# Decay rows of a chunked delta rule: broadcast transfers and a select on GpSimd in place of two bf16 matmuls

## The chip, the cores and the metric

The kernel runs on one core of a Trainium2 chip. Its time is the device time of one execution in microseconds (us). Three timed runs gave 1241.6, 1245.53 and 1245.56 us, so the median is 1245.53 us. One further execution was recorded by the hardware profiler, and all lines of the profile come from that one.

## The reference

One encoder layer on 1024 tokens of width 1024, all in float32. A normalised input goes through one projection, whose columns feed two groups of heads: windowed attention (8 heads) and a gated delta rule (4 heads of 128, run forward and backward over the sequence). Their outputs are concatenated, projected back and added to the input; then follow a squared-ReLU feed-forward block of width 4096 and a last norm. The change lies in the delta rule, which is computed in chunks:

```python
gc = jnp.cumsum(g, axis=-1)
decay = jnp.exp(jnp.where(causal, gc[..., :, None] - gc[..., None, :], -jnp.inf))
kk = jnp.einsum("bnhcd,bnhsd->bnhcs", k, k)
a_mat = jnp.where(strict, beta[..., :, None] * kk * decay, 0.0)
...
qk = jnp.einsum("bnhcd,bnhsd->bnhcs", q, k) * decay
```

So each chunk, head and direction needs a square matrix `decay`: the exponential of a cumulated log-decay of one token less that of another, zero on one side of the diagonal. The kernel uses chunks of 128 tokens.

## The kernel before

**The pieces.** The layer is one long program without loops at run time. `phases` calls generators, and `weave` merges two of them by weights, so that the work of one stands in program order between the work of the other. The order in which each engine gets its instructions is then worked out at build time, by a timeline simulation of the framework (`schedule_with_timeline_sim=True` where the kernel is built). Each engine executes its own list strictly in that order, and waits at an instruction whose inputs or buffers are not ready.

**Buffers.** Tiles are handed out from rings by tag. `pt` has 12 buffers of 128 x 512, `pg` 24 of 128 x 1024, `sc` 4, `wh` and `wl` 3 each for split weights. The PSUM tags `psA` and `psB` have 4 banks each: GEMM results go to `psA`, small products and transposes to `psB`.

**GEMMs.** `gemm` multiplies in three fp32r passes (L127 to L129), 24 matmuls of 128 x 512 for one result bank. The weights are split into a high part by ScalarE (L122) and a low part by GpSimd (L123). The results of the convolved projections are copied out of `psA` by ScalarE (L395), those of `proj_z` by a Silu on ScalarE (L464).

**The stage of the change.** After the k and q projections, `phases` weaves two streams:

```python
run(weave((chain(self.proj_conv(C_GV, "v"), self.proj_z(), self.proj_attn()), 145.0),
          (chain(self.prep(), self.eliminate(), self.diag_blocks(), self.invert(tt, (0, 1))), 100.0)))
```

The first is nothing but GEMMs with what follows them: the v heads with their five-tap convolution on VectorE (L374, L376), a Silu (L378) and transposes on TensorE (L415, drained by L455), then z, then the attention's k, v and q (L477, L488, L500 to L502). The second is `prep`: for each of 8 chunks `c` it makes the 4 heads' k-k and k-q products in two `psB` banks (L637, L639), and for each direction `d` a half step follows:

- two bf16 matmuls put the decay rows on all partitions, in a third `psB` bank `rows`: one with a selector `selb` against `grow`, which holds each cumulated row as three bf16 parts (L644), one that adds the mask of -1e30 through a bf16 identity (L645);
- ScalarE takes four exponentials with a per-partition bias from `rows` into `dec`, a `pt` tile (L649);
- VectorE makes `at` (also `pt`) from `dec` and the k-k product (L653), and ScalarE copies its diagonal blocks into `diag` (L658); `at` goes to DRAM by SyncE's queue (L660);
- VectorE multiplies `dec` by the k-q product (L661), and that goes to DRAM too (L662).

`eliminate` then works on all diagonal blocks with VectorE alone (L670 to L681), `diag_blocks` transposes (L690, L691), and `invert` multiplies the blocks together (its tiles are cleared by L716). After this weave come the attention, the scan and the feed-forward block.

**Where the rows come from.** At the end of `gates`, the cumulated log-decays are transposed into PSUM (L353), cut into three bf16 parts by ScalarE and VectorE (L356 to L361), written to the DRAM tensor `gcd` (L365) and read back into `grow` (L366). `setup2` makes the selector, the identity and the two masks on GpSimd (L168 to L177).

Of the kernel before, what the change touches and what calls it, by code (L numbers as in the profile page):

```python
# [11 lines left out]
BF16 = mybir.dt.bfloat16  # L12
AF = mybir.ActivationFunctionType
ALU = mybir.AluOpType
AX = mybir.AxisListType

P = 128
# [5 lines left out]
GH = 4  # L23
# [5 lines left out]
NEG = -1e30  # L29
# [48 lines left out]
class Block:  # L78
# [76 lines left out]
    def setup2(self):  # L155
        nc, io, c = self.nc, self.io, self.const
        t = lambda name, shape, dt=F32: c.tile(list(shape), dt, name=name)
        ones = t("ones", (P, P))
        nc.gpsimd.memset(ones, 1.0)
        self.ones = ones  # L160
        self.tri = []
        for d, (cm, step) in enumerate(((-1, 1), (1, -1))):
            u = t(f"tri{d}", (P, P))
            nc.gpsimd.affine_select(out=u, in_=ones, pattern=[[step, P]], compare_op=ALU.is_ge, fill=0.0,
                                    base=0, channel_multiplier=cm)
            self.tri.append(u)
        self.identb = t("identb", (P, P), BF16)
        nc.gpsimd.tensor_copy(out=self.identb, in_=self.ident)  # L168
        self.maskb = []
        for d in range(2):  # L170
            m = t(f"maskb{d}", (P, P), BF16)
            nc.gpsimd.tensor_scalar(out=m, in0=self.tri[d], scalar1=-1.0, scalar2=-NEG, op0=ALU.add, op1=ALU.mult)
            self.maskb.append(m)
        self.selb, self.zero = t("selb", (P, 16), BF16), t("zero", (P, 1))
        nc.gpsimd.memset(self.zero, 0.0)
        nc.gpsimd.tensor_tensor(out=self.selb, in0=self.ident[:, 0:16], in1=self.ident[:, 16:32], op=ALU.add)
        nc.gpsimd.tensor_tensor(out=self.selb, in0=self.selb, in1=self.ident[:, 32:48], op=ALU.add)  # L177
        self.dtb = t("dtb", (P, 8))
        nc.sync.dma_start(out=self.dtb, in_=io["gdn_dt_bias"].rearrange("o d h -> o (d h)").to_broadcast([P, 8]))
        self.alog = t("alog", (P, 8))  # L180
        nc.sync.dma_start(out=self.alog, in_=io["gdn_a_log"].rearrange("o d h -> o (d h)").to_broadcast([P, 8]))
        self.nsink = t("nsink", (P, 8))
        nc.sync.dma_start(out=self.nsink, in_=io["attn_sink"].to_broadcast([P, 8]))
        nc.gpsimd.tensor_scalar(out=self.nsink, in0=self.nsink, scalar1=-1.0, scalar2=None, op0=ALU.mult)
        self.ssk, self.irk, self.rk2 = (self.head.tile([P, GH, NT], F32, name=n) for n in ("ssk", "irk", "rk2"))
        self.ssq = t("ssq", (P, GH, NT))
# [118 lines left out]
    def gates(self, ps):  # L305

        nc = self.nc
        c = self.const
        mk = lambda name: c.tile([P, NT, 8], F32, name=name)
        tmp = lambda: self.small((P, NT, 8), bufs=6, tag="gt")  # L310
        vt = nc.vector
# [7 lines left out]
        au, z, z2, p = tmp(), tmp(), tmp(), tmp()  # L319
# [31 lines left out]

        tp = self.ps("psB", (64, P))
        nc.tensor.transpose(tp, gc2.rearrange("p c x -> p (c x)"), self.ident)  # L353
        rr = self.sc((64, 2, P))
        part = self.small((64, 3, P), bufs=1, tag="gparts", dt=BF16)
        nc.scalar.copy(out=part[:, 0, :], in_=tp)  # L356
        vt.tensor_copy(out=rr[:, 0, :], in_=part[:, 0, :])
        vt.tensor_tensor(out=rr[:, 1, :], in0=tp, in1=rr[:, 0, :], op=ALU.subtract)
        vt.tensor_copy(out=part[:, 1, :], in_=rr[:, 1, :])
        vt.tensor_copy(out=rr[:, 0, :], in_=part[:, 1, :])  # L360
        vt.tensor_tensor(out=part[:, 2, :], in0=rr[:, 1, :], in1=rr[:, 0, :], op=ALU.subtract)  # L361
        self.grow = c.tile([P, GH, P], BF16, name="grow")
        nc.gpsimd.memset(self.grow, 0.0)
        for r in range(3):
            nc.sync.dma_start(out=self.gcd[r], in_=part[:, r, :])  # L365
        nc.sync.dma_start(out=self.grow[0:48], in_=self.gcd.rearrange("r (a h) t -> (r a) h t", h=GH))  # L366
        self.cc, self.w2 = mk("cc"), mk("w2")

    def conv_silu(self, ct, raw, out):
# [260 lines left out]
    def prep(self):  # L630
        nc = self.nc
        self.diag = [self.pg((P, 32, 32)) for _ in range(2)]
        for c in range(NT):
            sl = slice(c * P, (c + 1) * P)
            gg, kq = self.ps("psB", (P, GH, P)), self.ps("psB", (P, GH, P))
            for h in range(GH):
                nc.tensor.matmul(gg[:, h, :], self.kT[h][:, sl], self.kT[h][:, sl], start=True, stop=True)  # L637
            for h in range(GH):
                nc.tensor.matmul(kq[:, h, :], self.kT[h][:, sl], self.qT[h][:, sl], start=True, stop=True)  # L639
            for d in range(2):  # L640
                dec, at = self.pt((P, GH, P)), self.pt((P, GH, P))
                rows = self.ps("psB", (P, GH, P))
                i = 2 * c + d
                nc.tensor.matmul(rows, self.selb[:, i:i + 1].to_broadcast([P, P]), self.grow, start=True, stop=False)  # L644
                nc.tensor.matmul(rows, self.identb, self.maskb[d].unsqueeze(1).to_broadcast([P, GH, P]),  # L645
                                 start=False, stop=True)
                for h in range(GH):
                    i = 4 * d + h
                    nc.scalar.activation(out=dec[:, h, :], in_=rows[:, h, :], func=AF.Exp,  # L649
                                         bias=self.ngc[:, c, i:i + 1])  # L650
                for h in range(GH):
                    i = 4 * d + h
                    nc.vector.scalar_tensor_tensor(out=at[:, h, :], in0=dec[:, h, :],  # L653
                                                   scalar=self.cc[:, c, i:i + 1], in1=gg[:, h, :],
                                                   op0=ALU.mult, op1=ALU.mult)
                for q in range(4):
                    r = slice(32 * q, 32 * q + 32)
                    nc.scalar.copy(out=self.diag[d][r, :, 4 * c:4 * c + 4].rearrange("p i h -> p h i"),  # L658
                                   in_=at[r, :, r])
                nc.sync.dma_start(out=self.atd[c, :, d], in_=at)  # L660
                nc.vector.tensor_tensor(out=dec, in0=dec, in1=kq, op=ALU.mult)  # L661
                nc.sync.dma_start(out=self.pd[c, :, d], in_=dec)  # L662
                yield 1.5
# [585 lines left out]
    def build(self):  # L1249
        tc, nc = self.tc, self.nc  # L1250
        with (
# [7 lines left out]
            d = lambda name, shape: dram.tile(list(shape), F32, name=name)  # L1259
            self.biasd = d("biasd", (8, 32, 512))[:]  # L1260
            self.hd, self.sd = d("hd", (NT, P, D))[:], d("sd", (DFF // 256, 7, P, HALF))[:]
            self.gcd = dram.tile([3, 64, P], BF16, name="gcd")[:]
            self.zd, self.mad = d("zd", (GH, P, SEQ))[:], d("mad", (NT, P, HALF))[:]
            self.qad = d("qad", (2, 4, P, SEQ))[:]
            self.ktd, self.qtd = d("ktd", (GH, P, SEQ))[:], d("qtd", (GH, P, SEQ))[:]
# [127 lines left out]
```

## Time and profile before

| | |
|---|---|
| runs | 1241.6, 1245.53, 1245.56 us |
| profiled execution | 1245.29 us, of which the span of the records is 1243.6 us |
| mean granted TensorE clock | 0.983 |
| TensorE matmul busy | 1179.3 us (95% of the span) |
| VectorE, ScalarE, GpSimd busy | 854.0, 620.9, 574.4 us |
| the 32 row matmuls L644 and L645 | first at 144.3, last at 213.1 us |
| the 64 exponentials L649 | first at 145.7, last at 216.1 us |

In the profile, PE is the matmul stream of TensorE and PEld its weight loads, DVE is VectorE, ACT ScalarE, POOL GpSimd and SP SyncE, which here issues most transfers. A queue's name with a q (SPq, ACTq) is the sequencer of that engine. `L644` is a line of the kernel file. Busy time of PE runs a little over, since matmuls overlap in the pipeline: the distance from start to start says what one costs.

### The profile page before, as it was taken

The numbers are of one execution on the slowest core, as the hardware profiler recorded it, in microseconds if no ns is written. First come the engines' busy times: TensorE is split into PE (matmuls) and PEld (weight loads), VectorE is DVE, ScalarE is ACT, GpSimd is POOL, SyncE is SP. The second block draws the span as 40 slices with busy tenths as digits, with TensorE's granted clock in tenths as the row PEclk, the third lists the DMA queues.
The fourth block names the chain that finished last, engine by engine and source line by source line (L and its number), as shares of the span: only waits on it lengthen the run. The fifth ranks groups of instructions, "written<-read, shape, count | busy, mean of one in ns | idle before, by whom it ended". The sixth has DMA issues, their size and how long they took to land. (4 is left out here: it accounts for less than half of the span.)

```text
span 1243.6 us, 18468 instructions
## 1 busy us (share of the span) xinstructions
PE 1179.3 (95%) x6482; PEld 962.8 (77%) x6482; DVE 854.0 (69%) x1466; ACT 620.9 (50%) x1347; POOL 574.4 (46%) x486
## 2 busy tenths in 40 slices
PE   6999999899879999997899999999999999999997
PEld 5788877778657778876788888888777888888885
DVE  4677667973378996677654453544579797887976
ACT  6455688354575752125464544545555433444343
POOL 5354312224422334234474535445365655665595
PEclk9999999899889999998999999999999999999999
DMA  6134344524746667222234444344679624434323
GB/s 240 52 117 141 104 167 140 180 81 135 172 145 172 168 220 263 96 83 84 86 120 154 151 153 144 144 158 147 214 263 320 235 84 155 152 133 138 98 89 136
DMA packets 121629, 187.62 MB, mean 151 GB/s; under 512 B 11043, under 2 KB 64416, under 8 KB 121537
## 3 DMA queue, kind: packets, MB, share of 16 engines
q1 hardware_dynamic: 96708, 152.58, 37.2%
q10 hardware_dynamic: 16381, 29.67, 6.2%
q0 software_dynamic: 8448, 4.20, 2.0%
q8 instruction: 51, 0.84, 0.3%
q14 instruction: 41, 0.34, 0.1%
HBM read 122.39 MB, written 63.49 MB: 149 GB/s over the span
## 5 line engine op out<-in xcount | busy, mean ns | idle before, releaser
L127 PE MATMUL psA<-pg,wh 128*128 128x512 f32 x416 | 164.8, 397 | 1.7 <-ACT pt L464 1.7
L129 PE MATMUL psA<-pg,wl 128*128 128x512 f32 x416 | 164.1, 395 | 0.0
L128 PE MATMUL psA<-pg,wh 128*128 128x512 f32 x416 | 163.7, 394 | 0.0
L123 POOL TENSOR_TENSOR wl<-wr,wh 128x512 fp32r<-128x512 f32 x44 | 66.7, 1536 | 159.6 <-ACT wh L122 129.4
L1168 DVE TENSOR_TENSOR pg<-pg 128x512 fp32r<-128x512 f32 x112 | 123.0, 1133 | 17.6 <-ACT pg L1167 17.6
L123 POOL TENSOR_TENSOR wh<-wr,wh 128x512 fp32r<-128x512 f32 x32 | 47.4, 1502 | 129.0 <-ACT wh L122 129.0
L128 PE MATMUL psA<-pg,pg 128*128 128x512 f32 x256 | 99.9, 392 | 0.4 <-POOL pg L123 0.3
L127 PE MATMUL psA<-pg,pg 128*128 128x512 f32 x256 | 99.3, 392 | 0.9 <-DVE pg L1213 0.9
L1085 ACT ACTIVATE pt<-pt 128x512 f32<-128x512 f32 x64 | 40.3, 632 | 119.3 <-DVE pt L1075 119.3
L129 PE MATMUL psA<-pg,pg 128*128 128x512 f32 x256 | 99.7, 390 | 0.0
L123 POOL TENSOR_TENSOR pg<-wr,pg 128x512 fp32r<-128x512 f32 x48 | 73.4, 1560 | 51.5 <-ACT pg L122 51.5
L127 PEld LDWEIGHTS psA<-pg,wh 128*128 128x128 f32 x416 | 78.6, 189 | 19.0 <-ACT pt L464 2.1
L128 PEld LDWEIGHTS psA<-pg,wh 128*128 128x128 f32 x416 | 78.6, 189 | 17.8 <-issue 0.9
L129 PEld LDWEIGHTS psA<-pg,wl 128*128 128x128 f32 x416 | 78.6, 189 | 16.8
L1167 ACT CAST pg<-pg 128x512 fp32r<-128x512 f32 x112 | 67.1, 620 | 40.4 <-DMA pg<-sd 29.3
L128 PE MATMUL psB<-pg,pg 128*128 128x512 f32 x192 | 74.9, 390 | 0.8 <-POOL pg L123 0.7
L129 PE MATMUL psB<-pg,pg 128*128 128x512 f32 x192 | 74.8, 390 | 0.2 <-DVE pg L1168 0.2
L127 PE MATMUL psB<-pg,pg 128*128 128x512 f32 x192 | 74.7, 389 | 0.0
L122 ACT CAST wh<-wr 128x512 fp32r<-128x512 f32 x76 | 43.6, 623 | 50.0 <-PE psA L128 30.0
L1075 DVE TENSOR_TENSOR pt<-psB,pt 128x512 f32<-128x512 f32 x39 | 26.9, 689 | 54.0 <-PE psB L129 29.5
L1075 DVE TENSOR_TENSOR pt<-psA,pt 128x512 f32<-128x512 f32 x39 | 26.8, 689 | 51.8 <-PE psA L129 36.3
L127 PEld LDWEIGHTS psA<-pg,pg 128*128 128x128 f32 x256 | 48.1, 188 | 12.6 <-DVE pg L1213 2.1
(395 smaller groups left out, 3265.3 us busy)
## 6 DMA issues: line engine op xcount, KB each, us to landing
sd<-pt ACTq DMA_DIRECT2D x112, 256.0 KB, 2.1
pg<-sd SPq DMA_DIRECT2D x112, 256.0 KB, 2.9
wr<-in_w_ffn_in SPq DMA_DIRECT2D x32, 512.0 KB, 3.6
wr<-in_w_in SPq DMA_DIRECT2D x22, 512.0 KB, 5.0
pg<-in_x SPq DMA_DIRECT2D x16, 512.0 KB, 6.7
wr<-in_w_ffn_out SPq DMA_DIRECT2D x16, 512.0 KB, 4.7
sc<-kvd SPq DMA_DIRECT2D x14, 512.0 KB, 6.0
kvd<-pt SPq DMA_DIRECT2D x16, 256.0 KB, 2.4
```

What stands on the lines that cost most here:

```text
L122: nc.scalar.copy(out=h, in_=raw)
L123: (eng or nc.gpsimd).tensor_tensor(out=l, in0=raw, in1=h.bitcast(F32), op=ALU.subtract)
L127: nc.tensor.matmul(ps, wh, xh, start=first, stop=False, skip_group_check=onto)
L128: nc.tensor.matmul(ps, wh, xl, start=False, stop=False, skip_group_check=onto)
L129: nc.tensor.matmul(ps, wl, xh, start=False, stop=last, skip_group_check=onto)
L1075: self.nc.vector.tensor_tensor(out=out, in0=in0, in1=in1, op=ALU.add)
L1085: self.nc.scalar.activation(out=c, in_=c, func=AF.Relu)
L1167: nc.scalar.copy(out=s[:, 0], in_=raw)
L1168: v.tensor_tensor(out=s[:, 1], in0=raw, in1=s[:, 0].bitcast(F32), op=ALU.subtract)
```

## The change

The masks, the bf16 identity, the selector and the tensor `grow` go away, and so does the cutting into three parts. The cumulated rows go to DRAM as they are, in float32. In each half step of `prep`, SyncE issues a transfer that reads the four heads' rows of one chunk and direction (2 KB) and writes them to all 128 partitions of `dec` (256 KB); GpSimd's `affine_select` then replaces one side of the diagonal by -1e30 in place, for the four heads in one instruction of 128 x 512; and the four exponentials work in place on `dec` in SBUF instead of reading PSUM. No third `psB` bank is used.

```diff
 def setup2
-        self.identb = t("identb", (P, P), BF16)
-        nc.gpsimd.tensor_copy(out=self.identb, in_=self.ident)
-        self.maskb = []
-        for d in range(2):
-            m = t(f"maskb{d}", (P, P), BF16)
-            nc.gpsimd.tensor_scalar(out=m, in0=self.tri[d], scalar1=-1.0, scalar2=-NEG, op0=ALU.add, op1=ALU.mult)
-            self.maskb.append(m)
-        self.selb, self.zero = t("selb", (P, 16), BF16), t("zero", (P, 1))
+        self.zero = t("zero", (P, 1))
         nc.gpsimd.memset(self.zero, 0.0)
-        nc.gpsimd.tensor_tensor(out=self.selb, in0=self.ident[:, 0:16], in1=self.ident[:, 16:32], op=ALU.add)
-        nc.gpsimd.tensor_tensor(out=self.selb, in0=self.selb, in1=self.ident[:, 32:48], op=ALU.add)
 def gates
         tp = self.ps("psB", (64, P))
         nc.tensor.transpose(tp, gc2.rearrange("p c x -> p (c x)"), self.ident)
-        rr = self.sc((64, 2, P))
-        part = self.small((64, 3, P), bufs=1, tag="gparts", dt=BF16)
-        nc.scalar.copy(out=part[:, 0, :], in_=tp)
-        vt.tensor_copy(out=rr[:, 0, :], in_=part[:, 0, :])
-        vt.tensor_tensor(out=rr[:, 1, :], in0=tp, in1=rr[:, 0, :], op=ALU.subtract)
-        vt.tensor_copy(out=part[:, 1, :], in_=rr[:, 1, :])
-        vt.tensor_copy(out=rr[:, 0, :], in_=part[:, 1, :])
-        vt.tensor_tensor(out=part[:, 2, :], in0=rr[:, 1, :], in1=rr[:, 0, :], op=ALU.subtract)
-        self.grow = c.tile([P, GH, P], BF16, name="grow")
-        nc.gpsimd.memset(self.grow, 0.0)
-        for r in range(3):
-            nc.sync.dma_start(out=self.gcd[r], in_=part[:, r, :])
-        nc.sync.dma_start(out=self.grow[0:48], in_=self.gcd.rearrange("r (a h) t -> (r a) h t", h=GH))
+        rr = self.small((64, P), bufs=1, tag="grows")
+        vt.tensor_copy(out=rr, in_=tp)
+        nc.sync.dma_start(out=self.gcd, in_=rr)
 def prep
             for d in range(2):
                 dec, at = self.pt((P, GH, P)), self.pt((P, GH, P))
-                rows = self.ps("psB", (P, GH, P))
-                i = 2 * c + d
-                nc.tensor.matmul(rows, self.selb[:, i:i + 1].to_broadcast([P, P]), self.grow, start=True, stop=False)
-                nc.tensor.matmul(rows, self.identb, self.maskb[d].unsqueeze(1).to_broadcast([P, GH, P]),
-                                 start=False, stop=True)
+                i = 4 * (2 * c + d)
+                src = self.gcd[i:i + 4].rearrange("(o h) t -> o (h t)", o=1)
+                nc.sync.dma_start(out=dec.rearrange("p h t -> p (h t)"), in_=src.to_broadcast([P, GH * P]))
+                nc.gpsimd.affine_select(out=dec, in_=dec, pattern=[[0, GH], [-1 if d else 1, P]],
+                                        compare_op=ALU.is_ge, fill=NEG, base=0, channel_multiplier=1 if d else -1)
                 for h in range(GH):
                     i = 4 * d + h
-                    nc.scalar.activation(out=dec[:, h, :], in_=rows[:, h, :], func=AF.Exp,
+                    nc.scalar.activation(out=dec[:, h, :], in_=dec[:, h, :], func=AF.Exp,
                                          bias=self.ngc[:, c, i:i + 1])
 def build
-            self.gcd = dram.tile([3, 64, P], BF16, name="gcd")[:]
+            self.gcd = d("gcd", (64, P))[:]
```

## The prediction

> **What bounds the kernel now.** I read the page's head first, then the busy time by stretches around the change.
>
> ```profile
> span 1243.6 us, 18468 instructions
> PE 1179.3 (95%) x6482; PEld 962.8 (77%) x6482; DVE 854.0 (69%) x1466; ACT 620.9 (50%) x1347; POOL 574.4 (46%) x486
> core 0: us, PE busy (x) PEld busy (x) DVE busy (x) ACT busy (x) POOL busy (x), PEclk, DMA share, GB/s
> 143.00:222.00 79.00, 74.82 (x400) 60.15 (x398) 59.77 (x108) 69.58 (x160) 23.30 (x20) 0.98 0.51 165
> 222.00:262.00 40.00, 39.26 (x166) 32.37 (x167) 37.81 (x68) 5.58 (x11) 4.45 (x3) 0.95 0.32 108
> 262.00:300.00 38.00, 35.43 (x562) 28.50 (x561) 18.56 (x28) 26.61 (x44) 16.26 (x17) 1.00 0.37 118
> 300.00:320.00 20.00, 20.00 (x89) 16.54 (x89) 3.08 (x5) 6.20 (x10) 10.48 (x9) 1.00 0.68 175
> ```
>
> TensorE is the bound of the kernel (95%), but not of every stage alike. In the stage of `prep` (143 to 222 us) ScalarE is busy 69.58 of 79 us, 88%, and TensorE idles 4.2 us. From 222 on ScalarE has little to do, VectorE runs the elimination (37.81 of 40 us), and TensorE is full with the GEMMs of z and the attention: they, not the elimination, set the end of the weave, for 300 to 320 us holds 20.00 us of TensorE after the first inversions are done. The next stage waits for them:
>
> ```profile
> 328.08 2.53 ACT L720 COPY pg<-sc 32x256 f32<-32x256 f32 x4 [6.01 <-POOL pg L716]
> ```
>
> L720 stood 6.01 us for a `pg` buffer's clearing, and `pg` is full of the GEMMs' operands until they end. So a microsecond that TensorE gains before 322 us is a microsecond of the kernel, as long as TensorE is not then stopped by something else. What would stop it is seen where the stage of `prep` ends:
>
> ```profile
> 219.93 1.12 PE L415 MATMUL psB<-ident,sc 128*128 128x128 f32 x4 [1.71 <-DVE pt L661]
> 222.74 0.79 PE L127 MATMUL psA<-pg,wh 128*128 128x512 f32 x1 [1.69 <-ACT pt L464]
> 223.33 0.63 PE L128 MATMUL psA<-pg,wh 128*128 128x512 f32 x1
> 223.75 0.63 PE L129 MATMUL psA<-pg,wl 128*128 128x512 f32 x1
> 220.79 1.28 ACT L464 ACT_TABLE_LOAD   x1
> 222.09 2.06 ACT L464 ACTIVATE pt<-psA 128x512 f32<-128x512 f32 x4
> 220.00:225.00 5.00, 3.31 (x9) 2.47 (x10) 4.10 (x6) 4.11 (x7) 1.40 (x3) 0.50 0.51 191
> ```
>
> Four Silus of z stand together at 222.09: TensorE had filled all four `psA` banks and waited until ScalarE, done with `prep`, came to drain them. After this idle time the granted clock is 0.50, and matmuls start 0.42 us apart instead of 0.23. The Trainium skill ("TensorE: Matmul & The Clock Gate", Part 1) says that the clock halves after an idle window of about 3.4 us and comes back after as much work; the trace agrees in kind (8 slow starts, some 1.6 us lost). By this rule a longer wait here would cost no more clock than this one.
>
> **The change part by part.**
>
> *Two matmuls fewer in each half step.* The rows of a pair of half steps:
>
> ```profile
> 144.29 0.38 PE L644 MATMUL psB<-grow,selb 128*128 128x512 bf16 x1
> ...
> 144.94 0.38 PE L645 MATMUL psB<-maskb,identb 128*128 128x512 bf16 x1
> 144.96 0.58 PE L127 MATMUL psA<-pg,wh 128*128 128x512 f32 x1
> 145.38 0.40 PE L128 MATMUL psA<-pg,wh 128*128 128x512 f32 x1
> 145.62 0.39 PE L129 MATMUL psA<-pg,wl 128*128 128x512 f32 x1
> ```
>
> From 144.29 to 145.38 stand four of them and one L127. The GEMM's own pace is 0.24 (145.38 to 145.62), so the four cost 0.85 us, 0.21 each; 32 of them 6.8 us. That is the ceiling on TensorE's side.
>
> *What ScalarE lets through.* It has to finish the same 64 exponentials and 64 copies before z's Silus, so the stage can't end before ScalarE does.
>
> ```profile
> L658 ACT COPY pg<-pt 32x128 f32<-32x128 f32 x64 | 26.8, 418 | 4.1 <-DVE pt L653 3.6
> L649 ACT ACTIVATE pt<-psB,ngc 128x128 f32<-128x128 f32 x64 | 17.6, 381 | 0.2
> L649 ACT ACT_TABLE_LOAD x5 | 6.4, 1283 | 3.2 <-issue 3.1
> ACT wh L122 <- issue: 1.5, 1, 1.5
> L421 ACT ACTIVATE scr<-psB x64: 260/291/390, 73.7 to 140.1; 128x128 f32<-128x128 f32 x64
> L908 ACT ACTIVATE scr<-dbl x32: 294/310/316, 462.1 to 579.5; 128x128 f32<-128x128 f32 x32
> ```
>
> Its 9.4 us of idle time (79 less 69.58) are 4.1 before L658, 3.2 before the exponentials, 1.5 before L122 and 0.6 of others. The 3.2 were a wait for rows that TensorE wrote only after a GEMM; a row that lies in SBUF ahead of time ends it. The 1.5 (weights' buffers that a GEMM held) should go with a TensorE that is ahead. Of the 4.1 I take half: with `rows` gone from `psB`, the exponentials of the next half step can fill the gap. Against it, the exponentials read SBUF: of two Squares of the same size the one from SBUF takes 310 ns and the one from PSUM 291, so 64 x 0.02 = 1.3 us more (between 0 and 1.3, taken whole). ScalarE's stage then is 69.6 + 1.3 + 2.0 + 0.6 = 73.5 us, 5.5 less than 79. The step is between 0 (all waits stay) and the ceiling of 6.8 plus the waits at the stage's end; I take 5.5, since this is the later of the two engines.
>
> *The select on GpSimd.* It is not in the trace at this size.
>
> ```profile
> 2.90 0.54 POOL L164 TENSOR_SCALAR_AFFINE_SELECT tri<-ones 128x128 f32<-128x128 f32 x2
> L716 POOL MEMSET pg<- x6: 955/956/972, 146.4 to 335.7; 128x1024 f32 x6
> L123 POOL TENSOR_TENSOR wl<-wr,wh 128x512 fp32r<-128x512 f32 x12 | 19.3, 1633 | 61.4 <-ACT wh L122 38.0 <-PE psB L639 23.5
> ```
>
> Two selects of 128x128 took 0.54 us together; four times 0.27 is 1.1 us for 128x512 as the upper end, half of a 128x1024 clear (0.48) the lower. I take 1.0, nearest to the row of the same operation: 16 us in a stage where GpSimd works 23 of 79, and stands 61.4 us before L123. So the engine has room, but its order is fixed: a select queued behind an L123 that waits (the longest single wait was 23.5 us, for L639) waits with it, and the exponential behind the select, and everything behind that on ScalarE. An L123 behind a select is late by 1 us, with a spare `wh` and `wl` buffer to cover it.
>
> *Beside VectorE.*
>
> ```profile
> 151.04 3.51 POOL L123 TENSOR_TENSOR wl<-wr,wh 128x512 fp32r<-128x512 f32 x2 [2.83 <-ACT wh L122]
> 151.28 2.12 DVE L376 SCALAR_TENSOR_TENSOR sc<-sc,cols,sc 128x1024 f32<-128x1024 f32 x1
> 148.97 1.28 DVE L376 SCALAR_TENSOR_TENSOR sc<-sc,cols,sc 128x1024 f32<-128x1024 f32 x1
> ```
>
> A convolution tap took 2.12 us beside GpSimd's subtraction and 1.28 alone. If each select costs VectorE up to 0.84 us, that is 13 us, against the 19 us that VectorE idles in the stage (79 less 59.77); I count nothing, and the price if the idle time lies elsewhere is what the slower rival holds. "GPSIMD Engine Reference" of the Trainium skill, section 8, says that GpSimd shares its SBUF interfaces with VectorE and contends with instructions of two SBUF inputs; L376 is one, and its row agrees. It speaks against the change.
>
> *The transfers.*
>
> ```profile
> L660 SPq DMA_DIRECT2D atd<-pt x16: 319/320/514, 150.4 to 217.5; - x16
> DMA to landing us min/median/max: 2.0/2.0/5.6
> wl<-in_norm_final_w SPq DMA_DIRECT2D x1, 512.0 KB, 4.7
> wr<-in_w_ffn_out SPq DMA_DIRECT2D x16, 512.0 KB, 4.7
> ```
>
> The 256 KB of L660 take 0.32 us to issue and 2.0 to land. A broadcast of one row to 128 partitions exists too, the last norm's weight: 512 KB in 4.7 us, as a plain load of that size. So a broadcast is no slower, and one takes 2.0 to 2.4 us. Sixteen add 16 x 0.32 = 5 us on SyncE's queue, which is mostly empty in this stage, and 4.2 MB to the 13 MB moved there (165 GB/s over 79 us, a DMA share of 0.51): hidden. How early they start decides whether the 2.0 us show.
>
> ```profile
> L518 SPq DMA_DIRECT2D rb<-in_rel_bias x1: 346/346/346, 15.0 to 15.0; - x1
> L520 SPq DMA_DIRECT2D pt<-in_onehot x1: 488/488/488, 100.7 to 100.7; - x1
> ```
>
> Two loads that stand side by side in the code and need no one's result: the one with a buffer of its own went out at 15.0 us, the one into `pt` at 100.7, when the earlier users of `pt` had had theirs. So `pt` is handed out in program order, and a broadcast will not run far ahead: `dec` of the next half step comes after `at` of this one. From the first L653 to the next: issue 0.32, landing 2.0, select 1.0, exponential 0.38, L653 0.34, together 4.0 us, while the half steps now follow each other every 4.8 us (77 us from 144 to 221, by 16). It fits with 0.8 us to spare, and ScalarE has the copies L658 (1.7 us) to do meanwhile. I count 0, with the price under the last rival.
>
> *The gates.* Five VectorE steps and one of ScalarE between two waits fall away, one copy and one transfer of four remain.
>
> ```profile
> 73.78 0.72 DVE L357 CAST sc<-gparts 64x128 f32<-64x128 bf16 x1 [2.63 <-ACT gparts L356]
> 76.22 0.28 DVE L361 TENSOR_TENSOR gparts<-sc 64x128 bf16<-64x128 f32 x1
> ```
>
> From the first to the end of the last are 2.7 us on VectorE, which goes on with the convolution of k right behind; the copy takes some 0.3, so 2.4 us earlier. The k products of L637 come only at 139 us, with GEMMs between: between 0 and 2.4, and I count 0, because TensorE, which sets that stage, had GEMMs to do meanwhile. The casts and masks of `setup2` lie in the first 5 us, when GpSimd waits for the first norm anyway: 0. The `sc` buffer that held the parts comes free for the convolution: 0.
>
> *The sum.* 5.5 us in the stage of `prep`, and nothing else. From 222 on everything moves earlier by it. The profiled execution took 1245.3 us (its span and 1.7 us around it), 0.2 under the median of the runs: 1245.3 - 5.5 = 1239.8, which I round to 1240.
>
> **The rivals.**
>
> *The whole gain.* With `psB` relieved (two banks free for L415) the v heads' transposes and z's Silus are served in time as well. Then go all 6.8 us, the idle time of the stage (4.2 us, of which some 4 lie between 215 and 223), and the 1.6 us of slow clock: 12.6 us, so 1232.7. For it: three of the four L415 groups there waited for L649, L653 or L661, that is for banks. Against: their last wait is for ScalarE, and that has its own floor.
>
> *Hidden.* TensorE comes 6.8 us earlier to the full `psA` banks and waits there, since ScalarE ends `prep` when it did. For it: 222.74 shows exactly this wait, and 4.1 + 0.6 us of ScalarE's idle time hang on VectorE, with 1.3 us more of work coming. Then the gain is within 1 us: 1245. That the broadcasts themselves are served slowly, so that nothing of the promised lead exists, ends here too, as long as ScalarE's waits don't grow.
>
> *Slower: ScalarE waits at the head of its queue for a select.* Place: the first L649 of each half step, behind SyncE, transfer and GpSimd; behind it in ScalarE's order stand L122, L395, L464, and for these wait TensorE's weights and `psA` banks. Price: with w us of wait in each of 16 half steps, ScalarE's stage is 69.6 + 1.3 + 16 w. It equals today's 79 at w = 0.5; that is the point from which it decides. At w = 0.9 it is 85.3, 6 us more than today, so 1251. For it: the chain has only 0.8 us to spare per half step if it runs from one `at` to the next, GpSimd's list has single waits of up to 23.5 us, and VectorE's slower taps lengthen the same chain. Against it: in SyncE's list the broadcast stands ahead of the L660 of the same half step, so that in time it can run nearly one half step ahead of what it is ordered behind.
>
> **How the numbers follow.** The forecast has 0.40 (its own range 1237 to 1241.5: the step between 8.5, with all ScalarE's waits gone, and the bound below), the whole gain 0.12, hidden 0.23, slower 0.25. A measurement of this kernel can tell about 0.3% from no change, 3.7 us, so the first two are faster (below 1241.8): 0.52. Hidden is the same: 0.23. The third is slower (above 1249.3): 0.25. The range goes from the whole gain with a little for the gates, 1232, to the slower case at its price, 1251; beyond lie half of that case's chance and little on the other side, under 0.2.
>
> **What would show it.** Right: in the profile after, the stage from the first L637 of `prep` to the first GEMM after the four Silus takes 74 us instead of 79; ScalarE is busy over 94% of it; the broadcast lands before ScalarE's previous instruction ends, so that no wait of L649 for GpSimd's select is among the longest; L720's wait for L716 is as long as before but 5 to 6 us earlier. The whole gain: no idle time of TensorE near the end of the stage and a granted clock of 1.00 there. Hidden: the wait of L127 for L464 grows to some 8 us. Slower: L649 waits for the select by more than 8 us in total, and L123 starts later against its L122 than before. What would make the prediction wrong altogether: that the order worked out at build time comes out otherwise, with more changes of ScalarE's table between exponential and Silu (1.28 us each, as at 220.79), or z's GEMMs put elsewhere; or that the elimination, not the GEMMs, sets the end of the weave.

## The result and the profile after

The changed kernel takes 1258.19 us (median of 4 runs, 1255.75 to 1261.59) against 1244.19 us for the kernel before beside it: a ratio of 1.0104, with a 95% interval of 1.0083 to 1.0126. It is 14 us slower where 5.5 us less were forecast. The profiled execution took 1258.7 us.

Busy times from the page's head and of the first three of the stretches shown of before, now of the changed kernel, and, of both kernels, of the 205 us from 95 to 300:

```profile
PE 1184.4 (94%) x6450; PEld 969.4 (77%) x6450; DVE 857.2 (68%) x1462; ACT 624.6 (50%) x1346; POOL 576.7 (46%) x496
core 0: us, PE busy (x) PEld busy (x) DVE busy (x) ACT busy (x) POOL busy (x), PEclk, DMA share, GB/s
143.00:222.00 79.00, 66.91 (x341) 55.98 (x340) 53.86 (x93) 59.93 (x133) 24.10 (x28) 0.94 0.60 182
222.00:262.00 40.00, 34.23 (x138) 27.64 (x137) 35.01 (x59) 14.06 (x30) 11.75 (x10) 0.85 0.51 166
262.00:300.00 38.00, 34.13 (x404) 27.57 (x403) 21.68 (x36) 21.37 (x36) 9.66 (x11) 0.91 0.31 95
95.00:300.00 205.00, 183.27 (x1112) 150.75 (x1111) 141.42 (x213) 120.29 (x287) 60.23 (x61) 0.93 0.46 144
95.00:300.00 205.00, 197.51 (x1363) 160.61 (x1362) 147.39 (x240) 126.48 (x327) 58.94 (x53) 0.98 0.41 133
```

The last line is the kernel before. There are 32 matmuls fewer, as meant (6450 for 6482). But ScalarE does 59.93 us of work in the 79 us in which it did 69.58, TensorE idles 12.1 us there instead of 4.2 and 5.8 instead of 0.7 in the next 40, and its clock falls to 0.94, 0.85 and 0.91 where it was 0.98, 0.95 and 1.00. The last diagonal copies start at 230.1 us instead of 220.4, the last step of the elimination at 271.1 instead of 261.3, the last norm's last multiplication (L1227, before L1246) at 1249.1 instead of 1236.0.

The new operations, the longest waits between 125 and 262 us, and ScalarE's group of exponentials between 135 and 232 us (busy us, mean ns of one, idle us in front); the line of L653 is the kernel before:

```profile
L625 SPq DMA_DIRECT2D pt<-gcd x16: 379/436/504, 133.7 to 221.0; - x16
DMA to landing us min/median/max: 3.7/4.0/4.7
L626 POOL TENSOR_SCALAR_AFFINE_SELECT pt<-pt x16: 634/635/1616, 137.7 to 225.9; 128x512 f32<-128x512 f32 x16
POOL pt L626 <- DMA pt<-gcd: 54.3, 13, 12.7
DVE pt L634 <- ACT pt L630: 25.6, 11, 7.2
DVE pt L653 <- ACT pt L649: 13.5, 6, 5.8
ACT pt L630 <- POOL pt L626: 11.1, 6, 8.0
PE psB L396 <- DVE pt L634: 7.0, 2, 3.6
L630 ACT ACTIVATE pt<-pt,ngc 128x128 f32<-128x128 f32 x64 | 20.5, 391 | 11.2 <-POOL pt L626 11.1
```

(L625 is the broadcast, L626 the select, L630 the exponential, L634 the product `at`, L639 the diagonal copies, L641 and L643 the two stores, L618 and L620 the k-k and k-q products, L396 the transposes.) Along the chain, GpSimd stands 54.3 us for the transfers, before 13 of the 16 selects; ScalarE 11.1 us for the selects; VectorE 25.6 us for the exponentials, where it was 13.5 before; and TensorE 7.0 us before the transposes, and 3.7 before k-k products, for VectorE's products, which read the `psB` banks that it needs. One wait of ScalarE makes 8.0 of the 11.1 us. Where it arises, by the timelines of SyncE, GpSimd and ScalarE:

```profile
138.26 0.81 SPq L506 DMA_DIRECT2D biasd<-pt  x1
139.13 0.45 SPq L625 DMA_DIRECT2D pt<-gcd  x1
141.62 1.34 SPq L641 DMA_DIRECT2D atd<-pt  x1
143.47 4.57 SPq L236 DMA_DIRECT2D wr<-in_w_in  x1
148.16 2.01 SPq L643 DMA_DIRECT2D pd<-pt  x1
150.23 0.42 SPq L625 DMA_DIRECT2D pt<-gcd  x1
151.68 0.64 POOL L626 TENSOR_SCALAR_AFFINE_SELECT pt<-pt 128x512 f32<-128x512 f32 x1 [8.55 <-DMA pt<-gcd]
152.35 1.28 ACT L630 ACTIVATE pt<-pt,ngc 128x128 f32<-128x128 f32 x4 [8.04 <-POOL pt L626]
```

L506 writes the attention's shift bias to DRAM, 512 KB out of 8 partitions. The mean busy share of the DMA engines in tenths and what they moved from 138 to 152 us (40 slices of 0.35 us), and the landing of the L641 issued in that time:

```profile
DMA  0000155974444446974444444454445897989987
GB/s 0 0 0 0 18 70 105 240 170 53 53 53 53 47 53 99 257 176 53 47 47 53 53 53 47 53 64 47 53 47 56 108 102 181 257 316 398 360 290 246
atd<-pt SPq DMA_DIRECT2D x1, 256.0 KB, 11.0
```

The select at 151.68 is the second of the sixteen, and its row is the broadcast issued at 139.13, right behind the write: it came 12.5 us after its issue. (The one issued at 150.23 had its select at 155.63. The 3.7 to 4.7 us above are of the landings that the view could tell, and this one is not among them.) The trace marks the landing of a transfer in sixteen parts; of this broadcast eight marks stand at 141.3 to 141.6 us and eight at 150.6 to 151.6, when the write ends too (its last marks stand at 150.0 to 151.0). So half of the row came only when the write was done.

For some 8 us little more than 50 GB/s moved in most slices, at four tenths of the engines' time. The store issued at 141.62 took 11.0 us to land, where 2.0 is the median, and SyncE stood 4.57 and 2.01 us at issues that take some 0.4 otherwise. The Trainium skill ("DMA: Bandwidth & Descriptors", Rules for kernel authors) says that a transfer whose outermost dimension has fewer than 16 entries stays on at most as many of the 16 engines; here it has 8, and the busy share of four to five tenths and the eight late marks agree. In the kernel before the same write went out at 140.0 us, with two weight loads next on the queue; their issue took 5.57 us there, but none of its engines' long waits is for a transfer.

### The profile page after: what moved, and what is told of

It is laid out like the page before. It is cut to its first block, busy times and chain, and to the rows that moved or that the text cites. A ratio compares the mean times of both kernels' runs of the same rounds, so it can differ in the third digit from the quotient of the medians.

```text
span 1256.9 us, 18423 instructions
## 1 busy us (share of the span) xinstructions
PE 1184.4 (94%) x6450; PEld 969.4 (77%) x6450; DVE 857.2 (68%) x1462; ACT 624.6 (50%) x1346; POOL 576.7 (46%) x496
## 4 chain that ended last, share of the span: by engine, by line
PE 70%; DVE 10%; issue 6%; ACT 5%; DMA 5%; POOL 3%; SPq 0%; POOLq 0%; ACTq 0%; DVEq 0%
PE psA L127 13%; PE psA L128 13%; PE psA L129 13%; PE psB L127 7%; PE psB L129 7%; PE psB L128 7%; PE psB L786 3%; DMA pg<-sd 1%; PE psA L572 1%; DVE pg L1149 1%; PE psA L560 1%; DVE wr L550 1%; DVE pt L1158 1%; ACT pg L701 1%; POOL pg L123 1%
## 5 line engine op out<-in xcount | busy, mean ns | idle before, releaser
L127 PE MATMUL psA<-pg,wh 128*128 128x512 f32 x416 | 166.5, 401 | 2.2 <-ACT pt L445 2.2
L128 PE MATMUL psA<-pg,wh 128*128 128x512 f32 x416 | 165.8, 399 | 0.0
L123 POOL TENSOR_TENSOR wl<-wr,wh 128x512 fp32r<-128x512 f32 x44 | 68.5, 1575 | 102.3 <-ACT wh L122 87.6
L123 POOL TENSOR_TENSOR wh<-wr,wh 128x512 fp32r<-128x512 f32 x32 | 47.4, 1500 | 129.6 <-ACT wh L122 129.6
L123 POOL TENSOR_TENSOR pg<-wr,pg 128x512 fp32r<-128x512 f32 x48 | 73.3, 1558 | 50.9 <-ACT pg L122 50.9
L127 PEld LDWEIGHTS psA<-pg,wh 128*128 128x128 f32 x416 | 80.0, 192 | 19.6 <-ACT pt L445 2.6
L128 PEld LDWEIGHTS psA<-pg,wh 128*128 128x128 f32 x416 | 80.0, 192 | 17.1
L127 PEld LDWEIGHTS psA<-pg,pg 128*128 128x128 f32 x256 | 48.0, 188 | 12.4 <-DVE pg L1194 2.1
```

What stands on the lines that cost most here:

```text
L123: (eng or nc.gpsimd).tensor_tensor(out=l, in0=raw, in1=h.bitcast(F32), op=ALU.subtract)
L127: nc.tensor.matmul(ps, wh, xh, start=first, stop=False, skip_group_check=onto)
L128: nc.tensor.matmul(ps, wh, xl, start=False, stop=False, skip_group_check=onto)
```

## The experiments

The theories at the start. **A**: the chain transfer, select, exponential stands in front of ScalarE since a row is asked for at most one half step ahead. **B**: the select's place in GpSimd's list, among the weights' low parts, makes the loss. **C**: the order worked out at build time came out worse, whatever the waits. Later came **D**: the shift bias's write on SyncE's queue makes the longest stall. Ratios are to the kernel before, run beside each.

**e1, rows that cost nothing.** No transfer and no select; the exponentials read a constant tile with a bias that keeps them finite.

```diff
-                nc.sync.dma_start(out=dec..., in_=src.to_broadcast([P, GH * P]))
-                nc.gpsimd.affine_select(out=dec, in_=dec, ...)
-                    nc.scalar.activation(out=dec[:, h, :], in_=dec[:, h, :], func=AF.Exp, bias=self.ngc[...])
+                    nc.scalar.activation(out=dec[:, h, :], in_=self.mask[d], func=AF.Exp, bias=self.negc[...])
```

> Leaves out the bringing of the rows: no transfer and no select; the exponentials read a constant mask tile in SBUF, with a bias that keeps them finite. Theory A (the chain of transfer and select stands in front of ScalarE's exponentials because it is started at most one half step ahead): with no chain the 6.8 us of matmuls show, 1238 us, and ScalarE's stage ends before 217 us. Theory B (what hurts is that the select shares GpSimd's in-order list with the weights' low parts): 1238 us too. Theory C (the order worked out at build time is a worse one, whatever the waits): 1250 us or more.

Measured: 1238.51 us, ratio 0.995 (0.9933 to 0.9967). Without the matmuls and with nothing in their place the kernel is 6.2 us faster (0.5% of 1246.27; between 4.1 and 8.3 by the interval). C falls as the whole cause: the loss needs the rows' arrival.

**e2, no select.** The broadcasts stay, the select goes (same bias as e1).

> The changed kernel without the select (the masking is left out, and the bias is another so that the exponentials stay finite); the broadcasts stay. Theory A: of some 5 us from issue to the first exponential the select is 0.64, so 1253 to 1257 us, and ScalarE waits for the broadcast itself. Theory B: GpSimd's list is free of the chain, so 1240 us. Theory C: within 2 us of 1258.

Measured: 1253.0 us, ratio 1.0064 (1.0047 to 1.008). The longest wait moves one link up the chain, from the select to the transfer itself:

```profile
ACT pt L628 <- DMA pt<-gcd: 11.3, 4, 7.3
```

So 5 of the 14 us hang on the select and more on the transfers. This speaks for A and against B as the main cause, and so does the changed kernel's own trace: before 13 of its 16 selects GpSimd stood idle for the transfer, so its list was not what held them.

**e3, a ring of their own.** Four buffers for the rows, taken from `pt` (12 to 8).

```diff
-                dec, at = self.pt((P, GH, P)), self.pt((P, GH, P))
+                dec, at = self.buf("dec", 4, (P, GH, P)), self.pt((P, GH, P))
```

> The changed kernel with dec in a ring of its own of 4 buffers (pt keeps 8), so that a broadcast need not come after the at tile of the half step before. Theory A: the first four broadcasts go out before 140 us, later ones some three half steps ahead; ScalarE's waits for the select (11.1 us) fall under 3, and the time is 1238 to 1244 us. Theory B: selects still share GpSimd's list, 1253 to 1258. Theory C: 1250 to 1260.

Measured: 1268.95 us, ratio 1.0198 (1.0169 to 1.0228), slower than any theory expected. The diagonal copies do end earlier than in the changed kernel (221.8 instead of 230.1 us), but the kernel ends 8.6 us later (the last norm's last multiplication at 1257.7); a `pt` of 8 stands where there were 12, and it serves the later stages too. Two things were changed at once, so this run decides nothing on A.

**e4, two half steps ahead.** The rows are in `pt` with its 12 buffers, as in the changed kernel, but each row's broadcast and select are traced two half steps earlier.

```diff
+        for n in range(2):
+            fetch(n)                      # broadcast and select of half step n
...
+                if 2 * c + d + 2 < 2 * NT:
+                    fetch(2 * c + d + 2)
+                dec, at = ready.pop(0), self.pt((P, GH, P))
```

> The changed kernel with the broadcast and the select of a half step written two half steps earlier in the program, all in the ring pt of 12 as before. Theory A: as with a ring of its own, 1238 to 1245 us, with ScalarE's waits for the select under 3 us. Theory B: 1253 to 1258. Theory C: 1250 to 1260.

Measured: 1249.47 us, ratio 1.0034 (1.0015 to 1.0054): most of the loss is gone. The last diagonal copies start at 216.4 us, 4 us earlier than in the kernel before, with one large wait of ScalarE left, in the same place:

```profile
139.00 0.81 SPq L506 DMA_DIRECT2D biasd<-pt  x1
139.86 3.85 SPq L621 DMA_DIRECT2D pt<-gcd  x2
ACT pt L641 <- POOL pt L622: 10.4, 4, 6.7
```

Of the two broadcasts right behind the write (L621 here) the first lands 12.4 us after its issue, and SyncE stands again, 4.57 us at a store. This led to D.

**e5, e6 and e8: the shift bias early.** `bias_rows` is called before the q projection, in the changed kernel (e5), with e4's lead (e6), and in the kernel before (e8, the control). (The texts below say "before the first projection", but the call stands behind that of k; and the first speaks of the third broadcast, where the late row is the second.)

```diff
+        self.bias_rows()
         run(self.proj_conv(C_GQ, "q"))
...
-        self.bias_rows()
```

> Theory D: the longest single stall of the preparation (8.0 us of ScalarE before an exponential) is the third broadcast standing on SyncE's queue behind the write of the shift bias, 512 KB from 8 partitions. Here that write goes out before the first projection instead. D expects the 8.0 us wait of the exponentials for the select to go and the time to fall by about 8, to about 1250. If instead each broadcast is late by its own lead (theory A alone), the time stays at 1256 to 1259 and the waits spread over other half steps.

> The changed kernel with both: broadcasts and selects given out two half steps earlier, and the shift bias written before the first projection. A and D together expect no wait of the exponentials above 2 us in the preparation and a time of about 1241 to 1243, 3 to 5 below the kernel before. If the select's work beside VectorE, or the buffers that the earlier rows hold, costs by itself, the time stays at 1246 or above.

> The kernel before, with the shift bias written before the first projection. Its exponentials read rows that TensorE makes, so no broadcast stands behind that write: D expects no change, 1244 to 1247. A gain here of several us would mean that the early write helps by itself, and then what it brings in the changed kernel says nothing of the broadcasts.

Measured: e5 1256.37 us, ratio 1.0064 (1.0042 to 1.0086); e6 1246.53, ratio 0.9994 (0.9974 to 1.0014); e8 1246.26, ratio 0.9996 (0.9978 to 1.0014). The control shows that the write's place means nothing to the kernel before. The other two gain 5 us each over the same kernel with the write in its place, less than D expected. In e5 no broadcast stands behind the write any more, ScalarE waits 1.4 us in all for selects, and the kernel is still 0.64% slower than the one before: the write is only a part. In e6 the list worked out at build time put the first broadcasts around the write again:

```profile
101.22 0.81 SPq L506 DMA_DIRECT2D biasd<-pt  x1
102.08 0.47 SPq L621 DMA_DIRECT2D pt<-gcd  x1
...
115.30 1.28 ACT L641 ACTIVATE pt<-pt,ngc 128x128 f32<-128x128 f32 x4 [5.59 <-POOL pt L622]
115.00:120.00 5.00, 0.00 (x0) 0.00 (x0) 0.00 (x0) 4.64 (x12) 0.34 (x3) 0.98 0.02 9
```

The row asked for at 102.08 came to its exponentials at 115.30; behind them on ScalarE stood a copy and a Silu of the q projection, and TensorE did nothing from 115 to 120 us (the last line). The stall had moved with the write.

**e7, as e6 without the select.**

> As the kernel with rows given out two half steps earlier and the early shift bias, but without the select: the masking is left out. It tells what the 32 selects cost once the rows are not late. If they cost only by the waits, it is within 1 us of the kernel with them; if they slow VectorE's taps beside them or hold GpSimd's list, it is 3 to 6 us faster, 1236 to 1239.

Measured: 1245.45 us, ratio 0.9987 (0.9968 to 1.0005), with e6 inside the interval. A select that is not waited for costs nothing that shows here.

**e9, e10 and e11: the whole shift bias late.** `bias_rows` (load, matmul, copy and write) at the head of `eliminate`: in the changed kernel (e9), with e4's lead (e10), in the kernel before (e11, the control). **e12**: broadcast three half steps ahead, select one, shift bias late.

```diff
     def eliminate(self):
         nc = self.nc
+        self.bias_rows()
```

> The shift bias written early only moved its 512 KB in front of another broadcast: the first broadcasts, issued 0.9 us behind it, again took 13.1 us to land, there and with the rows given out earlier. Here it is written after the preparation, where no broadcast is near; the rest is the changed kernel. If that write makes the longest stall (theory D), no select waits more than about 6 us for its rows and the time is 1249 to 1253. If the short lead alone makes the loss (theory A), 1256 to 1259.

> Rows given out two half steps earlier, and the shift bias written after the preparation: both causes taken away. A and D together expect no wait of the exponentials above 2 us in the stage and 1240 to 1243, 3 to 6 below the kernel before and 2 to 4 above the kernel whose rows cost nothing. If it stays at 1246 or above with those waits gone, the transfers and selects cost something that no wait for them shows.

> The kernel before with the shift bias written after the preparation: the control for the two kernels beside it. D expects no change, 1244 to 1248, since no exponential there waits for a broadcast. A fall of several us would mean that part of what the other kernels gain has nothing to do with the rows.

> Broadcasts given out three half steps ahead and the select only one, so that no select stands at the head of GpSimd's list waiting for a transfer; the shift bias after the preparation. If selects that wait there hold up the weights' low parts and so TensorE, this is 1 to 3 us below the kernel with both two half steps ahead. If not, it is the same or, since a row holds its buffer one half step longer, up to 3 us slower.

(The first of these texts gives 13.1 us as a landing. That number was GpSimd's idle time before a select; the row behind the write in e6 took 12.5 us from its issue to its select, the one in e5 was not behind it.)

Measured: e9 1257.03 us, ratio 1.0086 (1.0059 to 1.0112); e10 **1234.18**, ratio **0.9904** (0.9879 to 0.993); e11 1245.83, ratio 0.9995 (0.9979 to 1.0012); e12 1238.22, ratio 0.9936 (0.9913 to 0.9959). e10 is faster than both kernels. In its stage TensorE is nearly full (83.41 of 87 us) and at full clock, and no wait of an exponential for a select stands in ScalarE's list from 125 us on:

```profile
135.00:222.00 87.00, 83.41 (x448) 70.40 (x447) 76.77 (x138) 67.45 (x168) 34.19 (x33) 1.00 0.69 216
```

e12 is no better than e10, so a select at the head of GpSimd's list isn't what is left. e9 did not fall as D expects, but its edit brought a stall of its own: TensorE stood from 214.9 to 226.1 us before the bias's matmul, whose one-hot load SyncE issued only at 221.7.

```profile
PE psB L503 <- issue: 11.3, 1, 11.3
```

**e13 and e14: the write alone late.** The matmul and copy stay, into a buffer of their own, and the write is traced in `eliminate`: the changed kernel (e13), and with e4's lead (e14).

```diff
-        row = self.pt((8, 512))
-        nc.vector.tensor_copy(out=row, in_=ps[:8, :])
-        nc.sync.dma_start(out=self.biasd, in_=row.unsqueeze(1)...)
+        nc.vector.tensor_copy(out=self.brow, in_=ps[:8, :])
 def eliminate
+        nc.sync.dma_start(out=self.biasd, in_=self.brow.unsqueeze(1)...)
```

> The changed kernel, with nothing moved but the write of the shift bias (512 KB from 8 partitions): its matmul and copy stay where they were, into a buffer of their own, and the write goes out after the preparation. If the write makes the 8.0 us stall (theory D), the time falls by 4 to 8, to 1250 to 1254, and no stall of TensorE like the 11.3 us before the bias's matmul comes in its place. If the short lead alone makes the loss (theory A), 1256 to 1259.

> Rows given out two half steps earlier, and the write alone moved behind the preparation. A and D together expect about the time of the kernel with the whole shift bias late, 1233 to 1241, against 1249 with the write in its old place. If it stays near 1249, the gain of that kernel came from moving the one-hot load and matmul, not from the write.

Measured: e13 1260.19 us, ratio 1.0108 (1.0086 to 1.0131); e14 1253.24, ratio 1.0058 (1.0037 to 1.0079). Nothing gained. By SyncE's and ScalarE's timelines of e13 the write had not moved: nothing held it back but its data, so it was handed out as soon as these were there.

```profile
139.13 0.81 SPq L648 DMA_DIRECT2D biasd<-brow  x1
140.01 0.45 SPq L624 DMA_DIRECT2D pt<-gcd  x1
...
148.18 3.00 SPq L624 DMA_DIRECT2D pt<-gcd  x1
...
153.04 1.28 ACT L629 ACT_TABLE_LOAD   x1 [8.86 <-DMA pt<-gcd]
```

The row that ScalarE stood for is again the one issued right behind the write, at 140.01.

**e17 and e18: the write held back.** As e13 and e14, but GpSimd first copies the finished rows into a `pt` buffer that the preparation has to release, which puts the write behind the last broadcast.

```diff
 def eliminate
-        nc.sync.dma_start(out=self.biasd, in_=self.brow.unsqueeze(1)...)
+        row = self.pt((8, 512))
+        nc.gpsimd.tensor_copy(out=row, in_=self.brow)
+        nc.sync.dma_start(out=self.biasd, in_=row.unsqueeze(1)...)
```

> The kernel whose shift-bias write alone was traced after the preparation did not move it: the write is handed out as soon as its data are there, and it went out at 139.1 us again, between the first broadcast and the second. Here the finished rows are first copied by GpSimd into a buffer that the preparation has to release, so that the write stands behind the last broadcast on SyncE's queue; the matmul and the one-hot load stay in place. If the write makes the longest stall (theory D), the 8 to 9 us wait at about 145 us goes and the time falls by 4 to 8, to 1250 to 1255. If the short lead alone makes the loss (theory A), 1257 to 1260.

> The same with rows given out two half steps earlier. Against it stands the kernel with that lead and the write at 139 us, 1249 to 1253, and the one with that lead and the whole shift bias late, 1234. Theory D expects 1233 to 1241, since the write is then the whole difference; if it stays at 1248 or above, moving the one-hot load and the matmul made the gain.

Measured: e17 1248.51 us, ratio 1.0024 (1.0008 to 1.004); e18 1241.38, ratio 0.9971 (0.995 to 0.9991). The same stretch of e17:

```profile
144.24 0.38 SPq L236 DMA_DIRECT2D wr<-in_w_in  x1
144.67 0.51 SPq L624 DMA_DIRECT2D pt<-gcd  x1
...
151.49 1.28 ACT L629 ACTIVATE pt<-pt,ngc 128x128 f32<-128x128 f32 x4 [1.72 <-POOL pt L625]
```

The same issues take 0.3 to 0.5 us, and the wait of 8.86 is gone. Between e13 and e17 stands the place of one transfer (with a small copy and one `pt` buffer), and 0.84%, 10 us. D holds, next to A; but e5, where no row stands behind the write either, gained only 5.

**e15 and e16: what the rows still cost in e10.** e10 without the selects (e15), and e1 with the shift bias late (e16).

> The kernel with rows two half steps earlier and the shift bias late, without the selects: the masking is left out. If selects that nobody waits for are hidden, 1233 to 1235, as with them. If they slow VectorE's taps beside them or hold GpSimd's list, 3 to 6 us less, 1228 to 1231.

> No broadcasts and no selects (the exponentials read a constant tile, so the decay values and their masking are left out), shift bias late. If transfers and selects are hidden in the kernel with rows two half steps earlier, the same 1232 to 1236. If it is 4 us or more below that, they still cost that much there; if it stays at 1238 as with the shift bias in its old place, the late shift bias brings nothing by itself.

Measured: e15 1236.68 us, ratio 0.9922 (0.9904 to 0.994); e16 1240.81, ratio 0.9952 (0.9934 to 0.9971). Neither is faster than e10 (0.9879 to 0.993): rows that arrive in time cost nothing that can be measured. e16 is even slower, so the lists' order weighs as much here as what was looked for. The late shift bias brings nothing to a kernel without broadcasts (e1 0.995, e16 0.9952).

**The account.** By ratios: changed kernel 1.0104; the write out of the way 1.0064 (e5, 5 us) or 1.0024 (e17, 10 us); with the longer lead as well 0.9971 (e18), 6.6 us less than e17; the lead alone 1.0034 (e4), 8.7 us; rows at no cost 0.995. So the loss divides into the write's stall and the short lead, and either edit alone takes a part of it away. How much each is worth is known to some 5 us only: e5 and e17 both clear the write away and differ by that much, and no run isolates the order of the lists. e10 lies 0.67% below e18 although it moves only the bias's load and matmul besides, and below the kernel without rows. Its stage has a clock of 1.00 where e18 has 0.94, and TensorE stands 2.9 us for the v heads' Silus (L359) where e18 has 6.7; why its order came out better is left open.

What goes along with the time is TensorE's idle time, read as in the last two lines of the first fence. From 95 to 300 us it is 7.5 us in the kernel before and 21.7 in the changed one. Of the other changed kernels, e9 and e13 have 18.7 to 20.9 us; the seven with ratios from 0.9987 to 1.0064 have 12.5 to 16.8; the six at 0.9971 and below 5.9 to 9.4. Only e3 (18.4 us at 1.0198) stands outside this order. ScalarE's waits for rows do not go along: 11.1 us in the changed kernel, 11.0 in e17, 1.4 in e5.

## Why the prediction was wrong

*The matmuls* were sized rightly: 6.8 us, and e1 shows 6.2. They are no ceiling of what the change can bring, though: e10 is 12 us faster than the kernel before, with a clock of 1.00, as "the whole gain" (12.6 us) had it; how much of that is the order of the lists is open.

*ScalarE's stage* was the right place to look, but 5.5 us of gain became a stage that ends 9.7 us later. Its terms: the exponentials out of SBUF cost 0.01 us each more (391 against 381 ns), 0.6 us in all instead of 1.3. The idle time in front of them, which was to go, grew from 3.4 us to 11.3 (with the table loads).

*The select* was overpriced (0.635 us against 1.0), and VectorE's taps beside it lost little (mean 1460 ns instead of 1427). As a link of a late chain it still cost 5 us (e2).

*The transfers are the step that failed.* Three things in it were wrong. First the price: 2.0 to 2.4 us to land, the 2.0 from the row of a store, the 2.4 as half of a 512 KB load's 4.7. The broadcast takes 4.0, while the same view of before has loads of that size into SBUF at 2.9 to 6.7 us, the nearer rows:

```profile
wr<-zd SPq DMA_DIRECT2D x8, 256.0 KB, 2.9
pt<-pd SPq DMA_DIRECT2D x16, 256.0 KB, 6.7
```

Then the chain: "together 4.0 us ... It fits with 0.8 us to spare" counted one exponential and one product. The last half step of the changed kernel, by the five timelines:

```profile
220.60 0.32 SPq L643 DMA_DIRECT2D pd<-pt  x1
220.96 0.45 SPq L625 DMA_DIRECT2D pt<-gcd  x1
223.47 2.52 POOL L123 TENSOR_TENSOR wl<-wr,wh 128x512 fp32r<-128x512 f32 x2 [2.90 <-issue]
225.94 0.64 POOL L626 TENSOR_SCALAR_AFFINE_SELECT pt<-pt 128x512 f32<-128x512 f32 x1
226.61 1.28 ACT L630 ACTIVATE pt<-pt,ngc 128x128 f32<-128x128 f32 x4 [1.16 <-POOL pt L626]
227.05 1.22 DVE L634 SCALAR_TENSOR_TENSOR pt<-pt,cc,psB 128x128 f32<-128x128 f32 x4 [0.31 <-ACT pt L630]
```

From the issue at 220.96 to the finished `at` at 228.27 pass 7.3 us, of which the select stood some 1 us behind two L123, as B has it; and the issue itself stands right behind the `pd` store of the half step before. At a step of 4.8 us neither 7.3 nor 6.3 fits by one lead of a half step: with two (e4) the ratio falls from 1.0104 to 1.0034. Last the queue: SyncE's list was called "mostly empty", and no transfer in it was asked how long it holds the others. The shift bias's 512 KB stand just ahead of the stage in program order, their write went out at 140.0 us in the trace of before, and 5 us (e5) to 10 (e17) hang on it.

*The rival that came true* is "ScalarE waits at the head of its queue for a select", with 0.25 and 1251 us. Its sign, over 8 us of such waits, came: 11.1 us, 0.7 us per half step against a deciding 0.5. But it is one stall of 8.0 us and five small ones, not sixteen alike, and its price was too low: by its own formula 11.1 us make a stage of 82.0 us, 3 more than 79, or 1248. It counted ScalarE alone; e5, with 1.4 us of such waits, is still 0.64% slower. What cost the time is that TensorE stopped, 17.9 us in 143 to 262 us instead of 4.9, mostly for products of VectorE (L634) that came late. It also lost clock, for it stopped at several places:

```profile
154.06 1.16 PE L618 MATMUL psB<-dbl 128*128 128x128 f32 x8 [2.78 <-DVE pt L634]
...
228.33 1.97 PE L396 MATMUL psB<-ident,sc 128*128 128x128 f32 x8 [3.61 <-DVE pt L634]
232.45 0.79 PE L127 MATMUL psA<-pg,wh 128*128 128x512 f32 x1 [2.15 <-ACT pt L445]
```

After the last two waits the GEMM's matmuls start 0.43 us apart up to 237 us instead of 0.23. The prediction said of the clock that a longer wait would cost no more than the one at the stage's end; by the rule it drew on (the Trainium skill, "TensorE: Matmul & The Clock Gate", Part 1) each further idle window is paid for again, and the trace agrees: the granted clock is 0.82 in 157 to 171 us, behind the first of these stops, and 0.64 in 230 to 240, behind the other two, where the kernel before has 1.00 in both.

*What held:* TensorE's time sets the end of the kernel, and a broadcast that lands early is hidden (e10, e15). The end of ScalarE's stage does not set it: in e4 the diagonal copies end 4 us earlier than in the kernel before and the kernel is 0.34% slower, and in e3 they end 8.3 us earlier than in the changed kernel and it ends 8.6 us later. At the gates the first k-k product comes 2.1 us earlier (137.4 instead of 139.5 us), near the upper end of a term that was counted as 0; what it is worth no run shows. (And all four groups of L415 at the stage's end waited for a bank, not three.)

## What to carry to other kernels

Before a product from a fast engine is replaced by a transfer, write down the whole chain of one step, from the issue (and what stands ahead of it on its queue) to the last reader that frees the next buffer, and price the landing by loads of that size, not stores. If that chain is not well below the step's time, ask for the data two steps ahead. And look at the queue for one slow neighbour, such as a write out of few partitions: with this one behind the stage and the longer lead, 1% slower became 0.3% faster (e18), and 1% faster where the whole shift bias moved (e10), for a reason that stays open. And count the idle time of the engine that bounds the kernel, not the waits of the engine that the change touches. Whether the write itself could be spread over more engines was not tried.

## What the runs showed of the hardware that was not expected

A write of 512 KB out of 8 partitions to DRAM held the transfer rate near 50 GB/s for some 8 us, where 182 GB/s are the mean of the stage, and transfers issued behind it on the same queue landed in two halves: eight marks of sixteen 2 to 3 us after the issue, the others only when the write ended, 12.5 us after the issue for a broadcast instead of 4.0 and 11.0 for a store instead of 2.0. Even issuing became slow in that time: 4.57 us for a weight load that takes 0.38 in e17.
